# Down projection of a conv FFN: gate products of the finished accumulators moved from POOL to VectorE, and the second pair's weight blocks requested earlier

## The chip, the cores and the metric

The kernel runs on one core of one Trainium2 chip. The metric is the device time of one execution in microseconds (us), as a median over runs. The engines are named as in the profile: PE (TensorE, matrix products), PEld (its weight loads), DVE (VectorE), ACT (ScalarE), POOL (GpSimd) and SP (SyncE, which here only issues transfers). A DMA is a transfer between memory in HBM (also the kernel's own scratch there) and SBUF. PSUM holds the accumulators of PE, eight banks of 128 x 512 fp32.

## The reference, cut to what matters

One layer over 512 positions and 1024 channels, all in fp32. The part around the change is the second sub-layer and what closes it:

```
def _conv_ffn(h, w_up, conv_w, conv_b, w_down):
    z = h @ w_up                                   # 512 x 5632
    ...
    zc = conv_b + conv_w[0] * zp[:, 0:S]           # causal, width 3
    ...
    val, gate = jnp.split(zc, 2, axis=-1)
    return (jax.nn.silu(gate) * val) @ w_down      # 2816 -> 1024
...
y = _conv_ffn(h, w_up[l], conv_w[l], conv_b[l], w_down[l])
x = _layer_norm(ALPHA * x + gt_f[:, None, :] * y) * ln_f_g[l] + ln_f_b[l]
```

`gt_f` is a gate per channel, computed from the condition `c`. In the kernel it lies as two row tiles, `gt_f[0]` and `gt_f[1]` (128 x 512, the same row in all partitions; in the trace `gtf`).

## The kernel before, in words

Products in near fp32: each operand is split into a high part (a copy to fp32r by ACT, names ending in h) and a low part (the difference, by DVE, names ending in l). A product is hi x hi + lo x hi + hi x lo, three matrix products. In a sweep the products with the low part of the weights are called the rests; they come after the others (line 1599, against 1601 and 1602).

Up projection: 44 units (`m`) of 128 rows of `w_up`, two to a pass `i` (value and gate). ACT, DVE and POOL apply convolution, Silu (ACT, line 1582) and the product val x gate (POOL, line 1583). Two passes make a pair `p` of 256 rows of `w_down`, 11 pairs in all (`HP`). `first_left` and `other_lefts` make the left factors (`xa xs xh xl` for the first sweep, `yh yl ys` for the second; the latter go to scratch in HBM for nine pairs).

Down projection: a scheme with seven block products in place of eight per 2 x 2 blocks. The first sweep accumulates four of them over the pairs (`m1 m5 m6 m7`, two row halves each, eight banks), the second the other three (`m2 m3 m4`). The weights of a pair of the first sweep are two raw blocks of 128 x 512 (`db0`, `db1`: the outer ones, for `m1`, `m7`) and a wide one of 128 x 1024 (`da`: the inner one, for `m6`, `m5`). For each, SP requests the raw tile, ACT casts it (`dbh`, `dah`), DVE subtracts (`dbl`, `dal`, line 1514), PE multiplies. Cast and difference tiles have two buffers each, so a cast waits until PE is done with the block but one before. The second sweep has `dc` (wide) and `dd`, in the same way, for pairs 0 to 4; pairs 5 to 10 (`R2 = 6`) have their three blocks split ahead and kept (`second_weights`: raw tiles `dr`, results `d2.. d3.. d4..` with the pair's number). `reload` fetches a pair's left factors back from scratch into `z` tiles, on POOL's queue. The list `ahead` says which of these follow which pair of the first sweep, as space allows (`free`).

Between the sweeps the eight banks are summed into SBUF tiles `u1 u4 u3 c22` (`evacuate`). Each belongs to a quarter of the output: `fold` multiplies it by `gt_f` (POOL, line 1704) and adds it to ALPHA * x (`residual`, DVE, line 1696). The row statistics follow for those that are then complete (line 1701). The closing (`close`, `final`, `row_end`) ends `m2 m3 m4` with the six pairs kept, row half by row half, multiplies by the gate, adds, normalizes and stores.

A scheduler sets each engine's order: it issues in the order of its own timeline, within the program's data dependencies. `behind_split` forbids it to place work ahead of the last split recorded in `last_lo`. Engines work in order: an instruction that waits holds up all behind it.

Of the kernel before, what the change touches and what calls it, by code (L numbers as in the profile page):

```python
# [17 lines left out]
D = 1024  # L18
# [33 lines left out]
def trunk(ctx: ExitStack, tc: tile.TileContext, A, out):  # L52
# [1456 lines left out]
    def split_wide(parts, n, name):  # L1509
        hi = wp.tile([P, D], F32R, name=name + "h", tag="whi")  # L1510
        lo = wp.tile([P, D], F32R, name=name + "l", tag="wlo")
        for raw, c in parts:
            nc.scalar.copy(out=hi[:, c], in_=raw)
            nc.vector.tensor_tensor(out=lo[:, c], in0=raw, in1=f(hi[:, c]), op=ALU.subtract)  # L1514
        return hi, lo
# [20 lines left out]

    def first_weights(p):
        rb = [block(wdn_row(2 * p, lo_half), "db0"), block(t3_t[p], "db1")]
        ra = whole(wide_t[p], "da")
        wb_ = split_wide(zip(rb, (lo_half, hi_half)), D, "db")  # L1540
        wa_ = split_wide(((ra, slice(0, D)),), D, "da")
        return wb_, wa_

    held = [None]
    for i in range(NP):
        half = []
        for v in range(2):
# [9 lines left out]
            if m == 2 * NP - 1:  # L1557
                opening = first_weights(0)
            cc = C_CONV + 4 * m
# [12 lines left out]
            half.append(t)  # L1572
        val, gate = half
        if 3 <= i < 3 + KT:
            ada_wide_piece(3, i - 3)
# [57 lines left out]
    for i in range(R2 - 2):  # L1633
        ahead += [(second_weights, HP - R2 + 2 + i, act_t), (reload, i)]
    ahead.append((reload, R2 - 2))
    free = 1 + 6
    for p in range(HP - 1):
        wb_, wa_ = first_weights(p) if p else opening
        x = lefts1(p)
        sweep_step(p, (  # L1640
            (wb_, ((m1, x[1], lo_half), (m7, x[7], hi_half))),
            (wa_, ((m6, x[6], lo_half), (m5, x[5], hi_half))),
        ))
        for _ in range(2 if p else 0):
            need = 6 if ahead and ahead[0][0] is second_weights else 3
            if ahead and free >= need:
                work, *args = ahead.pop(0)
                work(*args)
                free -= need
        free += 4  # L1650
    p = HP - 1
    rb = [block(wdn_row(2 * p, lo_half), "db0"), block(t3_t[p], "db1")]
    ra = whole(wide_t[p], "da")
    ws1 = {
# [48 lines left out]
    def fold(t, n, u):  # L1703
        nc.gpsimd.tensor_tensor(out=u, in0=u, in1=gt_f[n], op=ALU.mult)
        residual(t, n, u)
# [10 lines left out]
    for p in range(HP - R2):  # L1716
# [8 lines left out]
        ))  # L1725
        if R2 - 1 + p < SPILLED:
            reload(R2 - 1 + p)
        if p == 0:
            fold_whole(0)
            fold_whole(1)  # L1730
        if p == 1:
            fold(0, 0, u1[0])
            fold(1, 0, u1[1])
        if p == 2:
            fold(0, 1, u4[0])
            fold(1, 1, u4[1])
            lnfg = row_tiles(4, h_t, "lnfg")
            lnfb = row_tiles(5, h_t, "lnfb")
        if p == 3:
            fold(2, 0, u3[0])  # L1740
            fold(3, 0, u3[1])
    second_weights(HP - R2, h_t, pad_t)
    closing = [HP - 5, HP - 4, HP - 2, HP - 1, HP - 3, HP - 6]

    def final(t, n, acc, op, slot):
        q = pt_t("fq")
        nc.vector.tensor_tensor(out=q, in0=acc, in1=gt_f[n], op=ALU.mult)  # L1747
        nc.vector.tensor_tensor(out=x1[t][n], in0=x1[t][n], in1=q, op=op)  # L1748
        statistics(t, slot, n)
# [45 lines left out]
    for t in range(2):  # L1795
        close(2, m2[t], t)
        final(t, 0, m2[t], ALU.add, 0)
        close(3, m3[t], t)
        final(t, 1, m3[t], ALU.add, 1)
        row_end(t, 2)  # L1800
        if t == 0:
            close(4, m4[0], 0)
            final(2, 0, m4[0], ALU.subtract, 1)
            row_end(2, 2)
# [114 lines left out]
```

## Time and profile before

| what | value |
|---|---|
| median of three runs | 954.65 us (954.14 to 956.67) |
| the profiled execution | 952.53 us, span of its instructions 950.8 us |
| mean granted PE clock | 0.994 |
| first sweep | 823 to 888 us |
| second sweep | 888 to 917 us |
| closing and output | 917 us to the end |

The span runs from the first to the last instruction. "Idle before" in brackets behind a row of the timeline says how long the engine stood still before it and what ended that. A number before an engine's name in a row is its start, then its duration. `x2` at a row's end means two instructions merged in one row. The rows that matter are shown where the prediction uses them.

### The profile page before, as it was taken

The numbers are of one execution on the slowest core, as the hardware profiler recorded it, in microseconds if no ns is written. First come the engines' busy times: TensorE is split into PE (matmuls) and PEld (weight loads), VectorE is DVE, ScalarE is ACT, GpSimd is POOL, SyncE is SP. The second block draws the span as 40 slices with busy tenths as digits, with TensorE's granted clock in tenths as the row PEclk, the third lists the DMA queues.
The fourth block names the chain that finished last, engine by engine and source line by source line (L and its number), as shares of the span: only waits on it lengthen the run. The fifth ranks groups of instructions, "written<-read, shape, count | busy, mean of one in ns | idle before, by whom it ended". The sixth has DMA issues, their size and how long they took to land. (4 is left out here: it accounts for less than half of the span.)

```text
span 950.8 us, 12652 instructions
## 1 busy us (share of the span) xinstructions
PE 925.1 (97%) x4456; PEld 779.7 (82%) x4456; DVE 683.8 (72%) x1048; ACT 409.0 (43%) x690; POOL 282.1 (30%) x340
## 2 busy tenths in 40 slices
PE   7999999999999999999999999999999999989796
PEld 6988888888888888888888889988888888778585
DVE  7966668546677798776375689588887656667868
ACT  4576555533324322133323434655444455555221
POOL 4741121122342154402154713022213221111704
PEclk9999999999999999999999999999999999999898
DMA  9823112134447996774576440155554444399832
GB/s 333 314 68 105 58 35 83 42 135 154 135 144 270 327 356 226 255 239 137 174 261 205 154 156 23 46 182 194 178 171 141 146 143 144 122 320 326 288 95 89
DMA packets 68303, 165.78 MB, mean 174 GB/s; under 512 B 9232, under 2 KB 12752, under 8 KB 68240
## 3 DMA queue, kind: packets, MB, share of 16 engines
q1 hardware_dynamic: 57024, 137.54, 43.2%
q0 software_dynamic: 10784, 26.89, 8.1%
q8 instruction: 35, 0.57, 0.2%
q10 hardware_dynamic: 432, 0.55, 0.2%
q14 instruction: 28, 0.23, 0.1%
HBM read 144.16 MB, written 20.78 MB: 173 GB/s over the span
## 5 line engine op out<-in xcount | busy, mean ns | idle before, releaser
L95 DVE TENSOR_TENSOR wupl<-wup,wuph 128x1024 fp32r<-128x1024 f32 x38 | 52.4, 1379 | 24.1 <-PE pzu L118 15.9
L1583 POOL TENSOR_TENSOR zc<-zc 128x512 f32<-128x512 f32 x22 | 29.7, 1349 | 131.5 <-ACT zc L1582 108.0
L94 ACT CAST wuph<-wup 128x1024 fp32r<-128x1024 f32 x38 | 40.1, 1054 | 46.4 <-PE pzu L116 33.8
L94 ACT CAST wbh<-wb 128x1024 fp32r<-128x1024 f32 x24 | 25.3, 1054 | 71.7 <-PE py L116 53.0
L985 POOL DMA_DIRECT2D wt<-wb x44 | 24.4, 556 | 78.3 <-DVE wb L981 73.3
L95 DVE TENSOR_TENSOR wgl<-wg,wgh 128x1024 fp32r<-128x1024 f32 x22 | 29.9, 1359 | 20.7 <-PE pg L118 9.9
L1561 ACT ACTIVATE zc<-pzu,cols 128x512 f32<-128x512 f32 x44 | 34.0, 778 | 21.0 <-PE pzu L118 16.6
L981 DVE TENSOR_TENSOR wb<-wb,wb 128x512 f32<-128x512 f32 x44 | 35.3, 806 | 6.1 <-DMA wb<-in_wdn 5.7
L856 DVE SCALAR_TENSOR_TENSOR ada<-adar,cact,ada 128x512 f32<-128x512 f32 x42 | 38.6, 960 | 0.0
L95 DVE TENSOR_TENSOR wbl<-wb,wbh 128x1024 fp32r<-128x1024 f32 x24 | 30.9, 1288 | 10.7 <-PE pg L118 5.3
L775 POOL TENSOR_SCALAR pe<-pe,mx 128x128 f32<-128x128 f32 (+3 forms) x32 | 17.0, 534 | 69.3 <-DVE mx L774 52.4
L94 ACT CAST wgh<-wg 128x1024 fp32r<-128x1024 f32 x22 | 23.3, 1059 | 32.6 <-PE pg L116 24.7
L1564 DVE SCALAR_TENSOR_TENSOR zc<-pzu,cols,zc 128x511 f32<-128x511 f32 x44 | 32.5, 743 | 5.0 <-ACT zc L1561 4.9
L1568 DVE SCALAR_TENSOR_TENSOR zc<-pzu,cols,zc 128x510 f32<-128x510 f32 x44 | 32.6, 744 | 0.7
L419 POOL TENSOR_TENSOR mg<-mg,th 128x512 f32<-128x512 f32 x16 | 28.5, 1778 | 12.7 <-DVE th L416 12.5
L1623 POOL DMA_DIRECT2D z<-ys x27 | 14.7, 545 | 52.3 <-PE pd L1602 24.3
L298 DVE SCALAR_TENSOR_TENSOR acc<-ada,cact,acc 128x256 f32<-128x256 f32 (+1 forms) x29 | 28.7, 990 | 1.0
L937 POOL TENSOR_TENSOR asum<-apad 128x527 f32<-128x527 f32 x8 | 12.3, 1543 | 54.6 <-ACT apad L932 28.0
L1582 ACT ACTIVATE zc<-zc 128x512 f32<-128x512 f32 x22 | 13.9, 631 | 24.2 <-DVE zc L1568 24.2
L1160 POOL TENSOR_TENSOR oraw<-oraw,gtt 128x512 f32<-128x512 f32 x6 | 9.6, 1612 | 42.2 <-DMA oraw<-in_wo 42.2
L1182 POOL TENSOR_TENSOR o<-o,gtt 128x512 f32<-128x512 f32 x10 | 17.9, 1809 | 12.4 <-DMA o<-in_wo 10.9
L771 ACT ACTIVATE pe<-sc,mx 128x128 f32<-128x128 f32 (+3 forms) x32 | 16.8, 528 | 8.7 <-DVE mx L769 7.5
(1570 smaller groups left out, 3247.6 us busy)
## 6 DMA issues: line engine op xcount, KB each, us to landing
wup<-in_wup SPq DMA_DIRECT2D x44, 512.0 KB, 3.5
wb<-in_wb SPq DMA_DIRECT2D x24, 512.0 KB, 3.8
adar<-in_ada SPq DMA_DIRECT2D x48, 256.0 KB, 4.2
wg<-in_wg SPq DMA_DIRECT2D x22, 512.0 KB, 3.5
wb<-in_wdn SPq DMA_DIRECT2D x44, 256.0 KB, 5.0
wt<-wb POOLq DMA_DIRECT2D x44, 256.0 KB, 3.8
z<-ys POOLq DMA_DIRECT2D x27, 256.0 KB, 6.1
ada<-in_ada1p SPq DMA_DIRECT2D x24, 256.0 KB, 4.8
```

Source lines behind the costliest of these rows:

```text
L94: nc.scalar.copy(out=hi[:, :n], in_=raw[:, :n])
L95: ins = nc.vector.tensor_tensor(out=lo[:, :n], in0=raw[:, :n], in1=f(hi[:, :n]), op=ALU.subtract)
L298: ins = nc.vector.scalar_tensor_tensor(out=acc, in0=src, scalar=cact[:, k : k + 1], in1=acc, op0=ALU.mult, op1=ALU.add)
L419: nc.gpsimd.tensor_tensor(out=merged[m], in0=merged[m], in1=th, op=ALU.add)
L856: nc.vector.scalar_tensor_tensor(out=acc[n], in0=src, scalar=cact[:, k : k + 1], in1=acc[n], op0=ALU.mult, op1=ALU.add,)
L981: ins = nc.vector.tensor_tensor(out=dst, in0=x, in1=y, op=op)
L985: nc.gpsimd.dma_start(out=dst, in_=src)
L1182: nc.gpsimd.tensor_tensor(out=halves[n], in0=halves[n], in1=gt[n], op=ALU.mult)
L1561: nc.scalar.activation(t, pz, AF.Identity, bias=cols[:, cc + 3 : cc + 4], scale=cols[:, cc + 2 : cc + 3])
L1564: nc.vector.scalar_tensor_tensor(out=t[:, 1:512], in0=pz[:, 0:511], scalar=cols[:, cc + 1 : cc + 2], in1=t[:, 1:512], op0=ALU.mult, op1=AL ...
L1568: nc.vector.scalar_tensor_tensor(out=t[:, 2:512], in0=pz[:, 0:510], scalar=cols[:, cc : cc + 1], in1=t[:, 2:512], op0=ALU.mult, op1=ALU.add,)
L1583: nc.gpsimd.tensor_tensor(out=val, in0=val, in1=gate, op=ALU.mult)
```

## The change

Four things, all from the last up unit on. The raw outer blocks of pair 1 are requested together with pair 0's, and their split is written ahead of the last Silu. In the first sweep the weights kept for the second start after pair 2 in place of pair 1, at most one pair's per step, and all but two of the reloads are written before the second sweep. The gate products of `fold` go from POOL to DVE; they are written behind each pair's rests by `behind_split` (five of the eight), and three accumulators of the first row half and of the third quarter (`u1[0]`, `u4[0]`, `u3[0]`) are no longer folded there: `final` adds the second-sweep accumulator to them, multiplies the sum and adds it to ALPHA * x, four DVE instructions where there were three. The norm's rows (`lnfg`, `lnfb`) lie in tiles of another pool.

```diff
--- before.py
+++ after.py
@@ -1511,7 +1511,8 @@
         lo = wp.tile([P, D], F32R, name=name + "l", tag="wlo")
         for raw, c in parts:
             nc.scalar.copy(out=hi[:, c], in_=raw)
-            nc.vector.tensor_tensor(out=lo[:, c], in0=raw, in1=f(hi[:, c]), op=ALU.subtract)
+            ins = nc.vector.tensor_tensor(out=lo[:, c], in0=raw, in1=f(hi[:, c]), op=ALU.subtract)
+        last_lo[:] = [ins.ins]
         return hi, lo
 
     def whole(src, name):
@@ -1534,12 +1535,19 @@
     def wdn_row(k, c):
         return A["wdn"][k * P : (k + 1) * P, c]
 
-    def first_weights(p):
-        rb = [block(wdn_row(2 * p, lo_half), "db0"), block(t3_t[p], "db1")]
-        ra = whole(wide_t[p], "da")
-        wb_ = split_wide(zip(rb, (lo_half, hi_half)), D, "db")
-        wa_ = split_wide(((ra, slice(0, D)),), D, "da")
-        return wb_, wa_
+    def outer_raws(p):
+        return [block(wdn_row(2 * p, lo_half), "db0"), block(t3_t[p], "db1")]
+
+    def outer_split(raws):
+        return split_wide(zip(raws, (lo_half, hi_half)), D, "db")
+
+    def inner_raw(p):
+        return whole(wide_t[p], "da")
+
+    def inner_split(raw):
+        return split_wide(((raw, slice(0, D)),), D, "da")
+
+    opening = {}
 
     held = [None]
     for i in range(NP):
@@ -1555,7 +1563,10 @@
                 pz = ps("pzu")
                 mm_chunk(pz, uh, ul, h2_hi, h2_lo)
             if m == 2 * NP - 1:
-                opening = first_weights(0)
+                raws = outer_raws(0)
+                inner = inner_raw(0)
+                raws1 = outer_raws(1)
+                opening[0] = outer_split(raws), inner_split(inner)
             cc = C_CONV + 4 * m
             t = pt_t("zc")
             nc.scalar.activation(
@@ -1571,6 +1582,8 @@
             )
             half.append(t)
         val, gate = half
+        if i == NP - 1:
+            outer1 = outer_split(raws1)
         if 3 <= i < 3 + KT:
             ada_wide_piece(3, i - 3)
         if i == 3 + KT:
@@ -1632,25 +1645,33 @@
     ahead = [(second_weights, HP - R2 + 1, h_t)]
     for i in range(R2 - 2):
         ahead += [(second_weights, HP - R2 + 2 + i, act_t), (reload, i)]
-    ahead.append((reload, R2 - 2))
+    ahead += [(reload, i) for i in range(R2 - 2, R2 + 1)]
     free = 1 + 6
     for p in range(HP - 1):
-        wb_, wa_ = first_weights(p) if p else opening
+        if p == 0:
+            wb_, wa_ = opening[0]
+        else:
+            wb_ = outer1 if p == 1 else outer_split(outer_raws(p))
+            wa_ = inner_split(inner_raw(p))
         x = lefts1(p)
         sweep_step(p, (
             (wb_, ((m1, x[1], lo_half), (m7, x[7], hi_half))),
             (wa_, ((m6, x[6], lo_half), (m5, x[5], hi_half))),
         ))
-        for _ in range(2 if p else 0):
-            need = 6 if ahead and ahead[0][0] is second_weights else 3
-            if ahead and free >= need:
-                work, *args = ahead.pop(0)
-                work(*args)
-                free -= need
+        wide = 0
+        while p > 1 and ahead:
+            weights = ahead[0][0] is second_weights
+            need = 6 if weights else 3
+            wide += weights
+            if free < need or wide > 1:
+                break
+            work, *args = ahead.pop(0)
+            work(*args)
+            free -= need
         free += 4
     p = HP - 1
-    rb = [block(wdn_row(2 * p, lo_half), "db0"), block(t3_t[p], "db1")]
-    ra = whole(wide_t[p], "da")
+    rb = outer_raws(p)
+    ra = inner_raw(p)
     ws1 = {
         c: split_block(raw, f"d{c}", h_t)
         for c, raw in ((1, rb[0]), (7, rb[1]), (6, ra[:, :512]), (5, ra[:, 512:]))
@@ -1701,7 +1722,7 @@
         return nc.vector.bn_stats(out=stats[t][:, slot, :], in_=x1[t][n][:, c])
 
     def fold(t, n, u):
-        nc.gpsimd.tensor_tensor(out=u, in0=u, in1=gt_f[n], op=ALU.mult)
+        nc.vector.tensor_tensor(out=u, in0=u, in1=gt_f[n], op=ALU.mult)
         residual(t, n, u)
 
     def fold_whole(t):
@@ -1723,29 +1744,30 @@
             (wc_, ((m2, x[2], lo_half), (m3, x[3], hi_half))),
             (wd_, ((m4, x[4], lo_half),)),
         ))
-        if R2 - 1 + p < SPILLED:
-            reload(R2 - 1 + p)
-        if p == 0:
-            fold_whole(0)
-            fold_whole(1)
-        if p == 1:
-            fold(0, 0, u1[0])
-            fold(1, 0, u1[1])
+        if R2 + 1 + p < SPILLED:
+            reload(R2 + 1 + p)
+        if p in (1, 2):
+            behind_split(fold_whole, p - 1)
         if p == 2:
-            fold(0, 1, u4[0])
-            fold(1, 1, u4[1])
-            lnfg = row_tiles(4, h_t, "lnfg")
-            lnfb = row_tiles(5, h_t, "lnfb")
+            lnfg = row_tiles(4, act_t, "lnfg")
+            lnfb = row_tiles(5, act_t, "lnfb")
         if p == 3:
-            fold(2, 0, u3[0])
-            fold(3, 0, u3[1])
+            behind_split(fold, 3, 0, u3[1])
+            behind_split(fold, 1, 0, u1[1])
+        if p == 4:
+            behind_split(fold, 1, 1, u4[1])
     second_weights(HP - R2, h_t, pad_t)
     closing = [HP - 5, HP - 4, HP - 2, HP - 1, HP - 3, HP - 6]
 
-    def final(t, n, acc, op, slot):
+    def final(t, n, acc, op, slot, u=None):
         q = pt_t("fq")
-        nc.vector.tensor_tensor(out=q, in0=acc, in1=gt_f[n], op=ALU.mult)
-        nc.vector.tensor_tensor(out=x1[t][n], in0=x1[t][n], in1=q, op=op)
+        if u is None:
+            nc.vector.tensor_tensor(out=q, in0=acc, in1=gt_f[n], op=ALU.mult)
+            nc.vector.tensor_tensor(out=x1[t][n], in0=x1[t][n], in1=q, op=op)
+        else:
+            nc.vector.tensor_tensor(out=q, in0=u, in1=acc, op=op)
+            nc.vector.tensor_tensor(out=q, in0=q, in1=gt_f[n], op=ALU.mult)
+            residual(t, n, q)
         statistics(t, slot, n)
 
     def row_end(t, count):
@@ -1794,13 +1816,13 @@
     last_product.clear()
     for t in range(2):
         close(2, m2[t], t)
-        final(t, 0, m2[t], ALU.add, 0)
+        final(t, 0, m2[t], ALU.add, 0, None if t else u1[0])
         close(3, m3[t], t)
-        final(t, 1, m3[t], ALU.add, 1)
+        final(t, 1, m3[t], ALU.add, 1, None if t else u4[0])
         row_end(t, 2)
         if t == 0:
             close(4, m4[0], 0)
-            final(2, 0, m4[0], ALU.subtract, 1)
+            final(2, 0, m4[0], ALU.subtract, 1, u3[0])
             row_end(2, 2)
     halves = (slice(0, 256), slice(256, 512))
     close(4, m4[1][:, :256], 1, halves[0])
```

On ACT, at the last up unit (`zc` from `pzu` is the unit's bias step, `zc<-zc` its Silu, `yh xs xh ys` the last pair's left factors); before:

```order
L1561 ACTIVATE zc<-pzu,cols 128x512
L1582 ACTIVATE zc<-zc 128x512
L1481 CAST yh_7686<-zc 128x512
L1458 CAST xs_7683<-se 128x256
L1479 CAST xh_7684<-sd 128x512
L1513 CAST dbh<-db_7729 128x512
L1513 CAST dah<-da 128x1024
L1458 CAST ys_7688<-se 128x256
L1513 CAST dbh<-db_7731 128x512
```

and now:

```order
L1572 ACTIVATE zc<-pzu,cols 128x512
L1513 CAST dbh<-db_7661 128x512
L1513 CAST dbh<-db_7663 128x512
L1595 ACTIVATE zc<-zc 128x512
L1481 CAST yh_7696<-zc 128x512
L1458 CAST xs_7693<-se 128x256
L1513 CAST dah<-da 128x1024
L1479 CAST xh_7694<-sd 128x512
```

Both outer casts of pair 1 moved ahead of Silu, its wide cast ahead of one left factor.

On ACT, a few pairs later (`d27h d37h d47h` are pair 7's kept blocks); before, from pair 2's wide cast:

```order
L1513 CAST dah<-da 128x1024
L1530 CAST d27h<-dr_7827 128x512
L1530 CAST d37h<-dr_7829 128x512
L1530 CAST d47h<-dr_7831 128x512
L1513 CAST dbh<-db_7851 128x512
L1513 CAST dbh<-db_7853 128x512
L1513 CAST dah<-da 128x1024
```

and now, from pair 3's outer casts:

```order
L1513 CAST dbh<-db_7827 128x512
L1513 CAST dbh<-db_7829 128x512
L1513 CAST dah<-da 128x1024
L1531 CAST d27h<-dr_7867 128x512
L1513 CAST dbh<-db_7891 128x512
L1513 CAST dbh<-db_7893 128x512
L1531 CAST d37h<-dr_7869 128x512
L1531 CAST d47h<-dr_7871 128x512
```

Pair 3's casts stood behind pair 7's kept blocks and now stand ahead of them; the two later kept blocks stand between pair 4's outer casts and its wide one.

On DVE, in the second sweep from the last sums of the evacuation on (`c_` is a c22 tile, `x_..` the residual, `std` the statistics); before:

```order
L1685 TENSOR_TENSOR u_8248<-pd_7699,u_8248 128x512
L1696 SCALAR_TENSOR_TENSOR x_00_5043<-x_00_5043,u_8238 128x512
L1684 TENSOR_TENSOR c_8274<-pd_7700,u_8263 128x512
L1685 TENSOR_TENSOR u_8253<-pd_7700,u_8253 128x512
L1696 SCALAR_TENSOR_TENSOR x_10_5047<-x_10_5047,u_8243 128x512
L1514 TENSOR_TENSOR dcl<-dc,dch 128x1024
L1531 TENSOR_TENSOR d25l<-dr_8484,d25h 128x512
L1514 TENSOR_TENSOR ddl<-dd,ddh 128x512
L1696 SCALAR_TENSOR_TENSOR x_21_5052<-x_21_5052,c_8268 128x512
```

and now:

```order
L1705 TENSOR_TENSOR c_8286<-pd_7710,u_8275 128x512
L1706 TENSOR_TENSOR u_8265<-pd_7710,u_8265 128x512
L1514 TENSOR_TENSOR dcl<-dc,dch 128x1024
L1514 TENSOR_TENSOR ddl<-dd,ddh 128x512
L1725 TENSOR_TENSOR c_8280<-c_8280,gtf_7075 128x512
L1717 SCALAR_TENSOR_TENSOR x_21_5052<-x_21_5052,c_8280 128x512
L1722 BN_STATS std_8245<-x_21_5052 128x6
L1532 TENSOR_TENSOR d25l<-dr_8478,d25h 128x512
L1514 TENSOR_TENSOR dcl<-dc,dch 128x1024
L1514 TENSOR_TENSOR ddl<-dd,ddh 128x512
```

Pair 1's split (the first `dcl` here) stood behind two residuals whose products came from POOL; now both residuals are later or in the closing, and the products (line 1725) stand behind a pair's splits.

## The prediction

> **What bounds the kernel now.** I read the page first, then the chain of waits from 640 us on, then the timelines of the engines around the waits it names.
>
> ```profile
> span 950.8 us, 12652 instructions
> ...
> PE 925.1 (97%) x4456; PEld 779.7 (82%) x4456; DVE 683.8 (72%) x1048; ACT 409.0 (43%) x690; POOL 282.1 (30%) x340
> ```
>
> ```profile
> PE pe L1599 <- DVE dcl L1514: 6.2, 1, 6.2
> ...
> PE pd L1601 <- ACT dbh L1513: 4.4, 2, 2.6
> ```
>
> TensorE (PE) is busy for 97% of the span, and in the last 310 us it waits three times: twice for ScalarE's split of a first-sweep block (dbh), once for VectorE's split of a second-sweep block (dcl). Between them it has no idle time, so a wait removed is time gained, unless another takes its place. The prices come from starts in PE's timeline:
>
> ```profile
> 823.18 0.39 PE L1601 MATMUL pd<-dbh,xa 128*128 128x512 f32 x1
> ...
> 830.61 0.50 PE L1601 MATMUL pd<-dbh,xa 128*128 128x512 f32 x1 [1.83 <-ACT dbh L1513]
> ...
> 836.58 0.39 PE L1601 MATMUL pd<-dbh,xa 128*128 128x512 f32 x1
> ...
> 844.79 0.50 PE L1601 MATMUL pd<-dbh,xa 128*128 128x512 f32 x1 [2.61 <-ACT dbh L1513]
> ...
> 855.98 0.39 PE L1601 MATMUL pd<-dbh,xa 128*128 128x512 f32 x1
> ...
> 888.62 0.39 PE L1601 MATMUL pe<-dch,z 128*128 128x512 f32 x1
> ...
> 892.70 0.39 PE L1601 MATMUL pe<-dch,z 128*128 128x512 f32 x1
> ...
> 901.75 2.07 PE L1599 MATMUL pe<-dcl,z 128*128 128x512 f32 x4 [6.17 <-DVE dcl L1514]
> ...
> 904.47 0.46 PE L1601 MATMUL pe<-dch,z 128*128 128x512 f32 x1
> ```
>
> These are starts of pairs 0, 1, 2, 3 and 5 of the first sweep, then pairs 0, 1 (its rests at 901.75) and 2 of the second. From 855.98 to 888.62 six pairs take 32.64, 5.44 each; from 888.62 to 892.70 a second-sweep pair takes 4.08. Against that pairs 0 and 1 lose 13.40 - 10.88 = 2.52, pair 2 to 3 loses 8.21 - 5.44 = 2.77, pairs 3 and 4 lose 11.19 - 10.88 = 0.31, and second-sweep pair 1 loses 11.77 - 4.08 = 7.69. All losses: 13.29 us.
>
> The last loss is the 6.17 wait and a slow restart: windows of four microseconds give the granted clock (PEclk) behind it.
>
> ```profile
> core 0: us, PE busy (x) PEld busy (x) DVE busy (x) ACT busy (x) POOL busy (x), PEclk, DMA share, GB/s
> 896.00:900.00 4.00, 0.00 (x0) 0.00 (x0) 4.00 (x2) 0.00 (x0) 4.00 (x4) 0.72 0.25 80
> 900.00:904.00 4.00, 2.25 (x5) 1.82 (x6) 4.00 (x5) 1.67 (x2) 2.76 (x5) 0.50 0.55 163
> 904.00:908.00 4.00, 4.00 (x18) 3.22 (x17) 4.00 (x7) 1.40 (x2) 1.08 (x2) 0.92 1.04 309
> ```
>
> At half clock the six rests took 2.72 instead of 1.36. Why the block was late stands in VectorE's timeline beside POOL's:
>
> ```profile
> 889.91 2.75 DVE L1696 SCALAR_TENSOR_TENSOR x<-x,u 128x512 f32<-128x512 f32 x1 [0.49 <-POOL u L1704]
> ...
> 893.79 5.71 DVE L1696 SCALAR_TENSOR_TENSOR x<-x,u 128x512 f32<-128x512 f32 x1
> 899.42 2.28 DVE L1514 TENSOR_TENSOR dcl<-dc,dch 128x1024 fp32r<-128x1024 f32 x1
> ...
> 902.82 0.68 DVE L1696 SCALAR_TENSOR_TENSOR x<-x,c 128x512 f32<-128x512 f32 x1
> 903.42 0.68 DVE L1696 SCALAR_TENSOR_TENSOR x<-x,u 128x512 f32<-128x512 f32 x1
> ...
> 904.63 1.20 DVE L1514 TENSOR_TENSOR dcl<-dc,dch 128x1024 fp32r<-128x1024 f32 x1
> ```
>
> ```profile
> 888.57 2.55 POOL L1704 TENSOR_TENSOR u<-u,gtf 128x512 f32<-128x512 f32 x2
> ...
> 892.74 1.31 POOL L1704 TENSOR_TENSOR c<-c,gtf 128x512 f32<-128x512 f32 x1
> 894.00 2.51 POOL L1704 TENSOR_TENSOR u<-u,gtf 128x512 f32<-128x512 f32 x2
> ...
> 897.68 2.92 POOL L1704 TENSOR_TENSOR u<-u,gtf 128x512 f32<-128x512 f32 x2
> ```
>
> The same residual takes 0.68 once POOL has stopped multiplying, but 2.75 and 5.71 while it multiplies. The split queued behind is itself slow (2.28 against 1.20) and ends at 901.70; PE's rests start at 901.75.
>
> **The change part by part.** *Products.* POOL loses eight multiplications; VectorE gets five of them in the second sweep and three in the closing. A VectorE product of two fp32 SBUF tiles with gtf is not in the trace. Its nearest row is the residual at 902.82, with as many operands of the same size: 0.68, the next one starting 0.60 later; the far end is 5.71, beside a multiplying POOL. I take 0.60, or 0.72 where an instruction needs the one before it, since POOL then multiplies nothing. The cover is VectorE's spare time in a pair: between pair 1's wide split and pair 2's come a 512-wide split 0.60, product 0.60, residual 0.72, statistics 0.72, the split d25l 0.60, and pair 2's wide split 1.20, which is 4.4 against PE's 4.08 (statistics taken as long as the residual). The next two rounds, up to pair 4's wide split, hold 3.9 and 4.8. So the lead counts. Pair 1's wide split follows ScalarE's cast of the same block:
>
> ```profile
> 891.31 1.05 ACT L1513 CAST dch<-dc 128x1024 fp32r<-128x1024 f32 x1 [6.89 <-PE pe L1602]
> ```
>
> It can end at 892.36 + 1.20 = 893.6 and is wanted after 12 of the pair's 18 products, at 892.70 + 2.72 = 895.4. Carried through the rounds, the leads are 1.9, 1.5, 1.7 and 1.0. VectorE stays ahead and the 7.69 goes.
>
> *Second pair's blocks.* ScalarE reached pair 1's dbh only behind a cast that waited for POOL:
>
> ```profile
> 828.29 0.62 ACT L1481 CAST yh<-zc 128x512 fp32r<-128x512 f32 x1 [1.46 <-POOL zc L1583]
> ...
> 829.95 0.61 ACT L1513 CAST dbh<-db 128x512 fp32r<-128x512 f32 x1
> ...
> 841.12 0.62 ACT L1530 CAST d27h<-dr 128x512 fp32r<-128x512 f32 x1 [4.42 <-DMA dr<-in_wdn]
> ...
> 844.12 1.13 ACT L1513 CAST dbh<-db 128x512 fp32r<-128x512 f32 x2
> ```
>
> Now both halves stand ahead of the last Silu. Their buffer is free after pair 0's first eight products (0.227 each), about 825.2, so they end at 826.3; PE wants them near 828. Silu, which waits behind them, moves by some 0.1, and with it POOL's product and the last pair's left factors, which PE needs 50 us later. Pair 1's dah, behind two of those casts, ends near 830.6 and is wanted 36 products after 823.18, at 831.3. On SP the two requests pass ahead of wide loads for pairs 1 and 2: two issues of some 0.5 (below, 1.13 for two), hidden, as pair 1's wide block is not cast before 829. The 2.52 goes.
>
> *Second-sweep weights later.* The 844.12 cast for pair 3 stood behind d27h, which waited 4.42 for a transfer. Now pair 3's casts stand ahead of d27h, pair 4's dbh behind it. Next to be late: PE reaches pair 4 at 823.18 + 4 x 5.44 = 844.9 and its wide block at 846.8, whose cast stands behind d47h. The requests cannot go out earlier than before, since they wait for raw tiles that the d26 to d46 splits free:
>
> ```profile
> 834.57 1.13 SPq L1524 DMA_DIRECT2D dr<-in_wdn  x2
> ```
>
> Here 6.55 passed from issue to use. With 7 to 8 for the third, d47h ends near 845.5 and the wide cast near 846.5: a lead of 0.3. The cost lies between nothing and the old 2.77. I take 0.7 for all narrow places of pairs 4 to 6, the 0.31 of today within it, because order and lead both say that at most a part comes back. On POOL's queue the last reloads lose the products in front of them; the last norm's rows move on SP behind the last blocks, where only output stores follow. Both cost nothing.
>
> *Closing.* Three accumulators get four dependent instructions instead of three.
>
> ```profile
> 921.11 0.69 DVE L1747 TENSOR_TENSOR fq<-pe,gtf 128x512 f32<-128x512 f32 x1 [5.60 <-PE pe L110]
> ...
> 930.39 1.44 DVE L1748 TENSOR_TENSOR x<-x,fq 128x512 f32<-128x512 f32 x1
> ...
> 937.43 0.69 DVE L1747 TENSOR_TENSOR fq<-pe,gtf 128x512 f32<-128x512 f32 x1 [0.54 <-PE pe L110]
> ```
>
> ```profile
> 929.99 1.29 POOL L1769 TENSOR_TENSOR x<-x,lnfb 128x512 f32<-128x512 f32 x1 [1.14 <-ACT x L1768]
> ```
>
> The first added one falls in PE's shadow (VectorE waits 5.60 around it). The other two push a queue that from 927 to the end idles only those 0.54: 2 x 0.72 - 0.54 = 0.9, and 0.2 for meeting POOL's remaining adds, as the 1.44 at 930.39 did (0.75 more than 0.69): 1.1 in all. Ends: 0.6 (pitch 0.60, no new meeting) and 2.4 (two new ones).
>
> By the Trainium skill, "SBUF — State Buffer", Who interferes with whom, a VectorE instruction with two SBUF inputs and a POOL instruction that reads SBUF exclude each other, the later one waiting to the end of the earlier. The 1.44 agrees; the 5.71 spans several multiplications and is longer than that rule gives. By it any of the three four-step chains that meets an add waits it out; that is rival (5).
>
> **Sum.** 13.29 - 0.7 - 1.1 = 11.5. The profiled execution took 952.53 (span 950.8 and 1.7 around it) and would take 941.0; the median, 954.65, lies 2.1 higher, so 943.1.
>
> **The rivals.** (1) The stall only moves: d47h lands late and pair 4 waits what pair 3 did. For it: a lead of 0.3 beside a wait of 4.42. Against: only half of pair 4 stands behind it. 2.77 in place of 0.7: 945.2.
> (2) Transfers become the limit.
>
> ```profile
> 824.00:908.00 84.00, 73.28 (x314) 58.98 (x313) 62.98 (x80) 40.32 (x63) 26.25 (x36) 0.96 0.91 304
> 844.00:872.00 28.00, 27.21 (x119) 22.29 (x120) 18.14 (x25) 17.47 (x27) 3.22 (x6) 1.00 1.00 351
> 884.00:896.00 12.00, 11.58 (x52) 9.24 (x50) 11.51 (x12) 2.62 (x4) 9.02 (x11) 1.00 1.13 397
> ```
>
> The 84 us move 25.5 MB at 304 GB/s (last column), at a 0.91 share. Of these some 1.5 MB can go before or after. The other 24 have 84 - 12.6 = 71.4 us; at the 351 held for 28 us they need 68.4. If only 304 is held they need 78.9: 950.2. I price the middle, 946.6.
> (3) VectorE falls behind in the second sweep: were each of its ten products and residuals 0.35 longer, 3.5 less the last lead of 1.0 would be lost: 945.6. The leads speak against it.
> (4) Slower than before: the long residuals were not POOL's doing but the transfers', which fill the engines just there (884 to 896: share 1.13, 397 GB/s). Then each of the ten in the second sweep costs the mean excess of the two, (2.07 + 5.03) / 2 = 3.55, and 35.5 - 1.0 come on top: 978. It ends above 954.65 from an excess of 1.3 each. Against it: the 5.71 runs on through 896 to 900, where the share is 0.25, and residuals take 0.68 again from 902.82 while the share climbs to 1.04; both long ones lie beside POOL's products. The Trainium skill, "SBUF — State Buffer", SBUF: two separate sides, has transfers and engines on separate ports; the rows at 896 and 904 agree.
> (5) The closing is dearer: all three four-step chains meet one of POOL's adds, which stay, at 0.75 each as at 930.39: 2.3 more, 945.4. For it: VectorE is full there. Against: one meeting stands in the trace for three adds beside it.
>
> **How the numbers follow.** Forecast 0.56, own range 941.3 to 944.7; rivals (1) 0.16, (2) 0.10, (3) 0.06, (4) 0.04, (5) 0.05; 0.03 for a change that takes its gain back elsewhere and ends within 0.3% (2.9 us, about what a measurement here tells from no change), where the far end of (2) also lies, 0.01. Range 940.8 to 947.5: below, all 13.29 less 0.6 and a run's scatter; above, rivals (1), (3) and (5) and the middle of (2). Faster 0.92, same 0.04, slower 0.04.
>
> **What would show it.** Right: no PE wait over 0.5 before pair 1, the residuals at 0.6 to 0.75, the second sweep's PE without a gap, granted clock 1.00 to the closing, the closing's first fq near 909. Wrong: a PE wait for dbh or dah at pair 4 with a cast on ScalarE waiting for dr (1); waits for z or dc transfers (2); PE waiting for dcl with POOL idle (3) or residuals above 2 (4); more than 2.4 us longer from first fq to the end (closing).

## The result, and the profile after

The changed kernel took 940.73 us (median of four runs, 940.67 to 941.47) against 955.66 for the kernel before beside it: a ratio of 0.9844, 95% interval 0.9822 to 0.9866. The forecast was 943.1 in a range from 940.8 to 947.5: the sign was right, the forecast 2.4 too high, and the median lies 0.07 below the range. Two later comparisons of the same pair gave 942.44 (ratio 0.9881, 0.9862 to 0.9901) and 940.73 (0.9857, 0.9837 to 0.9878). Over all twelve runs the median is 941.14 (939.85 to 944.20), over all 43 runs of the kernel before 954.07 (952.26 to 957.8): 12.9 less.

The page of the changed kernel:

```profile
span 939.0 us, 12633 instructions
...
PE 922.3 (98%) x4456; PEld 778.8 (83%) x4456; DVE 679.2 (72%) x1053; ACT 408.7 (44%) x690; POOL 270.1 (29%) x332
```

Its waits of PE from 640 us on (us in total, how often, the longest). There were three; one is left, for another block:

```profile
PE pd L1614 <- ACT dah L1513: 1.1, 1, 1.1
```

PE's timeline (L1614 and L1612 are 1601 and 1599 of before): starts of pairs 0, 5 and 6 of the first sweep with the wait in pair 5, then pairs 0 and 1 of the second sweep, pair 1's rests, pair 2, and the closing.

```profile
822.42 0.39 PE L1614 MATMUL pd<-dbh,xa 128*128 128x512 f32 x1
...
849.62 0.39 PE L1614 MATMUL pd<-dbh,xa 128*128 128x512 f32 x1
...
853.63 0.50 PE L1614 MATMUL pd<-dah,xh 128*128 128x512 f32 x1 [1.12 <-ACT dah L1513]
...
856.50 0.39 PE L1614 MATMUL pd<-dbh,xa 128*128 128x512 f32 x1
...
883.70 0.39 PE L1614 MATMUL pe<-dch,z 128*128 128x512 f32 x1
...
887.78 0.39 PE L1614 MATMUL pe<-dch,z 128*128 128x512 f32 x1
...
890.50 1.07 PE L1612 MATMUL pe<-dcl,z 128*128 128x512 f32 x4
...
891.86 0.39 PE L1614 MATMUL pe<-dch,z 128*128 128x512 f32 x1
...
903.65 0.39 PE L108 MATMUL pe<-d26l,z 128*128 128x512 f32 x1
```

Five pairs take 27.20, that is 5.44 a pair: pairs 0 to 4 together lose nothing. Pair 5 takes 6.88 and loses 1.44. In the second sweep each pair takes 4.08, and pair 1's rests follow at once. VectorE there:

```profile
887.48 1.23 DVE L1514 TENSOR_TENSOR dcl<-dc,dch 128x1024 fp32r<-128x1024 f32 x1 [1.78 <-ACT dch L1513]
...
889.23 0.68 DVE L1725 TENSOR_TENSOR c<-c,gtf 128x512 f32<-128x512 f32 x1
889.94 0.69 DVE L1717 SCALAR_TENSOR_TENSOR x<-x,c 128x512 f32<-128x512 f32 x1
...
892.01 1.22 DVE L1514 TENSOR_TENSOR dcl<-dc,dch 128x1024 fp32r<-128x1024 f32 x1
...
908.38 0.69 DVE L1768 TENSOR_TENSOR fq<-u,pe 128x512 f32<-128x512 f32 x1 [4.16 <-PE pe L110]
...
918.98 1.66 DVE L1717 SCALAR_TENSOR_TENSOR x<-x,fq 128x512 f32<-128x512 f32 x1
```

A product takes 0.68, a residual 0.69. Pair 1's split ends at 888.71, 1.8 before it is wanted at 890.50 (forecast: 1.9). The granted clock (third column from the end) stays at 1.00; the last column has the GB/s that the transfers move:

```profile
884.00:888.00 4.00, 4.00 (x19) 3.31 (x18) 2.22 (x4) 1.30 (x2) 1.78 (x4) 1.00 1.21 397
888.00:892.00 4.00, 4.00 (x19) 3.33 (x18) 3.90 (x6) 2.47 (x4) 1.74 (x4) 1.00 1.03 298
892.00:896.00 4.00, 4.00 (x20) 3.30 (x19) 3.93 (x8) 1.57 (x2) 0.94 (x2) 1.00 1.09 355
```

The span divides at three starts in the timelines of PE and VectorE: pair 0 of the first sweep, pair 0 of the second, and the closing's first fq.

| kernel (number of profiled executions) | start of first sweep | first sweep | second sweep to first fq | fq to end |
|---|---|---|---|---|
| before, the one shown | 823.18 | 65.44 | 32.49 | 29.69 |
| before, mean of 5 | 823.66 | 65.54 | 32.99 | 29.70 |
| after, the one shown | 822.42 | 61.28 | 24.68 | 30.62 |
| after, mean of 3 | 822.99 | 61.02 | 24.68 | 30.61 |
| products alone | 822.65 | 64.49 | 24.68 | 30.58 |
| opening alone | 823.01 | 60.76 | 33.17 | 29.76 |
| ahead alone | 823.71 | 65.33 | 33.80 | 29.66 |

The means differ by 12.6: 4.5 in the first sweep, 8.3 in the second, 0.9 given back in the closing, and 0.7 ahead of the first sweep, where the program is the same and its start varies from 822.4 to 824.8 between executions.

### The profile page after: what moved, and what is told of

Same layout as the page of the kernel before. It is cut to its first block, busy times and chain, and to the rows that moved or that the text cites. A ratio compares the mean times of both kernels' runs of the same rounds, so it can differ in the third digit from the quotient of the medians.

```text
span 939.0 us, 12633 instructions
## 1 busy us (share of the span) xinstructions
PE 922.3 (98%) x4456; PEld 778.8 (83%) x4456; DVE 679.2 (72%) x1053; ACT 408.7 (44%) x690; POOL 270.1 (29%) x332
## 4 chain that ended last, share of the span: by engine, by line
PE 97%; DVE 1%; POOL 0%; ACT 0%; DMA 0%; issue 0%; POOLq 0%; SPq 0%; ACTq 0%
PE pzu L115 7%; PE pzu L116 7%; PE pzu L118 7%; PE py L115 5%; PE py L116 5%; PE py L118 5%; PE pg L115 4%; PE pg L116 4%; PE pg L118 4%; PE lat L528 2%; PE pd L1614 2%; PE pd L1612 2%; PE pd L1615 2%; PE pa L115 2%; PE pu L115 2%; PE pu L116 2%
```

## The experiments

**The parts alone.** Three kernels are the kernel before with one part of the diff each; a fourth is the kernel before again. Only the gate products on VectorE, with `final` and the norm's rows:

```diff
-        nc.gpsimd.tensor_tensor(out=u, in0=u, in1=gt_f[n], op=ALU.mult)
+        nc.vector.tensor_tensor(out=u, in0=u, in1=gt_f[n], op=ALU.mult)
...
+            behind_split(fold_whole, p - 1)
```

> The kernel before with the third part alone: the gate products on VectorE behind each pair's rests, three of them in the closing; the first sweep as before. Both theories take the second sweep's loss (7.7 us in the profile of before) away and add 0.9 in the closing. Theory A (the 2 to 3 us by which the runs of before exceed its profiled run, and their spread of 3.7 us, are VectorE held up by POOL's products for a time that differs from run to run): 9 to 10 us faster in the median and runs within 1 us of each other. Theory B (they come from transfers landing at other times in the first sweep): 6.8 us faster, and the spread of before stays.

Only pair 1's outer blocks (`raws1`, `outer1`):

```diff
+                raws1 = outer_raws(1)
...
+            outer1 = outer_split(raws1)
```

> The kernel before with the second pair's raw blocks requested and split ahead of the last Silu, nothing else. Both theories: PE's wait before pair 1 goes, 2.5 us faster. Theory A: the runs spread as those of before do (3 us or more). Theory B: part of the spread goes.

Only the list and loop of the second-sweep weights, with the reloads:

```diff
-    ahead.append((reload, R2 - 2))
+    ahead += [(reload, i) for i in range(R2 - 2, R2 + 1)]
...
+        while p > 1 and ahead:
```

> The kernel before with the kept second-sweep weights one pair later and the reloads moved ahead, nothing else. Both theories: PE's wait of 2.6 us before pair 3 goes, up to 2.8 us faster; less if, as in the changed kernel, a kept block's transfer holds ScalarE up at a later pair (1.1 us there). Theory A: the spread of before stays. Theory B: the spread goes, since the wait for that transfer is where it comes from.

And the kernel before, once more:

> The kernel before once more, for a second profile of it. Theory A: the starts of the first sweep's pairs agree with the first profile to 0.3 us, and the second sweep's loss differs from 7.7, between 8 and 13 us if this run is slower. Theory B: the losses differ before pair 5, and the second sweep loses 7.7 again.

Beside 953.88 for the kernel before they took 945.34 (ratio 0.9908, 0.9891 to 0.9925), 949.34 (0.9950, 0.9935 to 0.9965), 953.78 (1.0001, 0.9989 to 1.0013), and the copy 954.38 in one run: 8.5, 4.5 and 0.1, together 13.1 against the 12.9 of the whole. The parts add up, and one of them is worth nothing that these runs show. The 8.5 of the products lies between the 6.8 of theory B and the 9 to 10 of theory A. With them alone PE has one wait left from 640 us on:

```profile
PE pd L1602 <- ACT dbh L1513: 1.8, 1, 1.8
```

The one at pair 3 is absent there, as it is in three of the five profiled executions of the kernel before; these have one of 0.91 to 1.03 at pair 4 in its place, and why this kernel has none no run says. With the opening alone the one for dcl stays, and both for dbh are gone, pair 3's too:

```profile
PE pe L1611 <- DVE dcl L1514: 6.3, 1, 6.3
PE pd L1613 <- ACT dah L1513: 0.6, 1, 0.6
```

ScalarE's timeline of that kernel gives the reason: pair 3's wide cast now stands ahead of d27h, though `ahead` is as before.

```profile
838.62 1.05 ACT L1513 CAST dah<-da 128x1024 fp32r<-128x1024 f32 x1 [0.18 <-PE pd L1614]
842.98 0.62 ACT L1530 CAST d27h<-dr 128x512 fp32r<-128x512 f32 x1 [3.30 <-DMA dr<-in_wdn]
```

With pair 1's blocks earlier, the scheduler puts pair 3's casts ahead of d27h by itself. With "ahead" alone it does not: pair 3's casts still stand behind d47h, as in the kernel before.

```profile
843.05 0.62 ACT L1530 CAST d47h<-dr 128x512 fp32r<-128x512 f32 x1 [0.43 <-DMA dr<-wt]
843.58 1.14 ACT L1513 CAST dbh<-db 128x512 fp32r<-128x512 f32 x2
```

In the copy the third wait is 6.17 again, to the hundredth, so a varying hold-up between VectorE and POOL was not what spreads the runs; pair 2 to 3 lost 3.63 there against 2.77.

**Nothing from "ahead".** The changed kernel with the list, loop and reloads of before, beside the changed kernel itself:

```diff
-    ahead += [(reload, i) for i in range(R2 - 2, R2 + 1)]
+    ahead.append((reload, R2 - 2))
```

> The changed kernel without its part on the second-sweep weights (the list and loop of before, reloads as before). ScalarE's order is then that of the changed kernel, row for row; three reloads on POOL's queue and the norm's rows on SP stand elsewhere. Theory O: the earlier blocks of pair 1 alone remove the wait of pair 3, and this part adds nothing: 940.7, within 0.5 of the changed kernel, and one PE wait near 1.1 at pair 5. Theory of the prediction: this part removes the 2.77, so it comes back: 943.5, with a PE wait above 2 at pair 3.

> The changed kernel again, in more runs, for the step that added 2.1 us to the profiled execution's forecast. Theory W: the runs of the kernel before differ because ScalarE stands in order behind transfers that land at other times from run to run, and with those waits gone the runs lie close: median 940.4 to 941.2, all of ten runs or so within 1.5 us. Theory S: the four runs so far lay close by chance; more runs spread as those of the kernel before do (3.8 us over 17 runs), with a median of 941.5 to 943.1.

942.04 (940.7 to 942.84) and 942.44 (940.8 to 944.2). Theory O holds: PE waits for dah once, 1.5 and 0.8, and nothing comes back at pair 3. The first sweep with the old list took 62.00, against 60.55 to 61.81 in eight profiled executions that have the new one and the opening, so some tenths from this part are not excluded. And theory S holds: the first four runs lay close by chance.

**The wait that is left.** The casts and differences of the kept weights written behind the next pair's split:

```diff
+        for args in pending:
+            behind_split(second_splits, *args)
...
+            if weights:
+                pending.append((*args, second_raws(args[0])))
```

> The changed kernel with the casts and differences of the kept second-sweep weights written behind the next pair's split; their raw tiles are requested where they were. Theory: the 1.12 us that PE still waits at pair 5 comes from dah standing behind d38h, which waits 2.04 for its transfer; with d38h behind the next pair's outer casts it goes: 939.6, no PE wait over 0.3 in the first sweep. Rival: the raw tiles are held for a pair longer, so later requests go out later and the wait turns up elsewhere: 940.7 to 943.

941.39 (941.11 to 943.52). The wait did not go, it changed its block:

```profile
PE pd L1614 <- ACT dbh L1513: 0.9, 1, 0.9
```

**The engine or the place.** First the products on VectorE where the kernel before had them on POOL; then the reverse, the five of the second sweep on POOL in the new places.

```diff
-        if p in (1, 2):
-            behind_split(fold_whole, p - 1)
+        if p == 0:
+            fold_whole(0)
+            fold_whole(1)
...
```

> The changed kernel with the gate products on VectorE, but written where the kernel before had them (not held behind a pair's split), and a closing of three steps throughout. Theory E (POOL's multiplications made the residuals long): residuals and products 0.60 to 0.75 throughout, though the order is worse: counted at 0.6 each, pair 1's dcl ends 0.6 late, its ddl 1.5 more, pair 2's dcl and ddl 1.0 and 1.6 more, 4.7 in all, less 0.9 in the closing: 944.5. Rival T (the transfers there made them long): residuals of 2 to 5 us again, a wait of 6 or more for dcl: 947 or above.

```diff
-        nc.vector.tensor_tensor(out=u, in0=u, in1=gt_f[n], op=ALU.mult)
+        nc.gpsimd.tensor_tensor(out=u, in0=u, in1=gt_f[n], op=ALU.mult)
```

> The changed kernel with the five products that stand in the second sweep back on POOL, in their new places behind a pair's split; the closing stays at three four-step chains. If places alone did it: 941 to 942. If the engine counts: each residual waits for its product on POOL (1.3 each) with the next pair's split behind it, and the splits beside a product are longer; the leads of 0.9 to 1.8 are used up in one to three rounds: 942.5 to 946, with PE waits for dcl.

The first took 944.99 (0.9913, 0.9896 to 0.9930), as theory E counted. Its VectorE works without a gap, products and residuals 0.6 apart:

```profile
890.72 1.22 DVE L1514 TENSOR_TENSOR dcl<-dc,dch 128x1024 fp32r<-128x1024 f32 x1
...
894.87 1.29 DVE L1717 SCALAR_TENSOR_TENSOR x<-x,u 128x512 f32<-128x512 f32 x2
```

and PE still waits 2.2 for dcl: 0.20 before pair 1's rests, since five products and two residuals stand ahead of that split, and 1.97 before pair 2's, which has three more products and four residuals in front of it. The transfers are as dense there (last column) as beside the long residuals of the kernel before, whose same two windows move 403 and 388 GB/s:

```profile
888.00:892.00 4.00, 3.80 (x18) 2.82 (x16) 4.00 (x7) 1.72 (x3) 1.60 (x3) 1.00 1.18 381
892.00:896.00 4.00, 4.00 (x17) 3.06 (x18) 4.00 (x7) 1.68 (x2) 1.10 (x3) 1.00 1.19 399
```

The second took 944.26 (0.9890, 0.9870 to 0.9910); VectorE's first wide split there, beside four multiplications:

```profile
889.37 4.00 DVE L1514 TENSOR_TENSOR dcl<-dc,dch 128x1024 fp32r<-128x1024 f32 x1 [1.78 <-ACT dch L1513]
```

Neither (the opening alone) took 949.34, engine alone 944.99, place alone 944.26, both 941.14: the whole gain takes both. (The second has the shorter closing of before, worth 0.9; in the third the three products of the closing stay on VectorE.)

**POOL's multiplications by themselves.** The changed kernel with eight multiplications added on POOL that nobody waits for:

```diff
+        if p == 0:
+            beside = h_t("beside", F32)
+            for i in range(8):
+                nc.gpsimd.tensor_tensor(out=beside, in0=u4[0], in1=gt_f[i % 2], op=ALU.mult)
```

> The changed kernel with eight multiplications of 128x512 on POOL added in the second sweep (u4 of the first row half by gtf, into a spare tile that nobody reads, no wait of any other instruction on them). VectorE's instructions and their order up to pair 3 stay. If POOL's multiplications are what held VectorE: products, residuals and wide splits beside them take 2 to 6 us in place of 0.68 and 1.2; in the kernel before three of them took 8.2 more, the leads here are 1.4 to 1.8, so PE waits 3 to 7 for dcl: 944.5 to 948.5. If not (the transfers, or only the order): all at 0.6 to 1.3, no PE wait over 0.5 in the second sweep, 941 to 942.

947.29 (947.15 to 947.35; 0.9925, 0.9908 to 0.9942), 6.2 above the 941.14 of the changed kernel, and 6.0 of it between the second sweep's start and the first fq (30.72 against 24.68). VectorE, then POOL:

```profile
888.07 2.42 DVE L1514 TENSOR_TENSOR dcl<-dc,dch 128x1024 fp32r<-128x1024 f32 x1 [1.78 <-ACT dch L1513]
...
895.78 2.28 DVE L1514 TENSOR_TENSOR dcl<-dc,dch 128x1024 fp32r<-128x1024 f32 x1
...
899.67 1.76 DVE L1725 TENSOR_TENSOR c<-c,gtf 128x512 f32<-128x512 f32 x1
901.47 1.66 DVE L1717 SCALAR_TENSOR_TENSOR x<-x,c 128x512 f32<-128x512 f32 x1
```

```profile
888.09 1.31 POOL L1752 TENSOR_TENSOR beside<-u,gtf 128x512 f32<-128x512 f32 x1
...
893.99 8.58 POOL L1752 TENSOR_TENSOR beside<-u,gtf 128x512 f32<-128x512 f32 x5
```

Each of these VectorE instructions became about one multiplication longer (1.0 to 1.2). That shows that POOL's multiplications hold VectorE up and make PE wait. It does not yet show the 5.71: here the two engines took turns, in the unbroken row of five from 893.99 on too. All eight write one tile, so the next run gave them four tiles in turn:

```diff
-            beside = h_t("beside", F32)
+            beside = [h_t(f"beside{i}", F32) for i in range(4)]
```

> As the run with eight multiplications added on POOL, but they write four tiles in turn, so that none waits for the one ahead of it, and the first four stand without a request between them. Theory of the gap: in the run before each wrote the same tile, which left a gap after each in which VectorE came in, so the instructions alternated (1.7 to 2.4 each); without it the wide split of pair 1 waits for several, as the residuals of 5.71 and 6.73 did: 4 to 6 for it, 945 to 949. Rival: they alternate again, 2.3 to 2.5 for that split, and the long residuals come from their own kind of instruction: near 947.3.

948.73 (948.13 to 949.23; 0.9935, 0.9901 to 0.9969). The same split, then POOL beside it:

```profile
888.23 6.02 DVE L1514 TENSOR_TENSOR dcl<-dc,dch 128x1024 fp32r<-128x1024 f32 x1 [1.78 <-ACT dch L1513]
894.17 1.78 DVE L1514 TENSOR_TENSOR ddl<-dd,ddh 128x512 fp32r<-128x512 f32 x1
```

```profile
886.00 5.03 POOL L1752 TENSOR_TENSOR beside<-u,gtf 128x512 f32<-128x512 f32 x4
...
891.61 1.27 POOL L1752 TENSOR_TENSOR beside<-u,gtf 128x512 f32<-128x512 f32 x1
...
893.97 3.11 POOL L1752 TENSOR_TENSOR beside<-u,gtf 128x512 f32<-128x512 f32 x2
```

By the Trainium skill, "SBUF — State Buffer", Who interferes with whom, a VectorE instruction with two SBUF inputs and a POOL instruction that reads SBUF exclude each other: the later one waits for the end of the earlier. The 1.0 to 1.2 of the run that took turns agree, since one multiplication takes 1.3; the 6.02 does not. The theory of the gap holds for this split: where no multiplication waits for the one ahead of it, VectorE can stay out for several (1.23 became 6.02). How many is open. It stayed out of the pause from 891.03 to 891.61, in which POOL issued a request; but the next split, 1.78 in place of 0.69, came in between the two multiplications from 893.97, though neither waits for the other. Requests of POOL by themselves cost nothing: in the changed kernel two of them run from 891.87 to 892.94 beside the split of 1.22 at 892.01.

**Closing.** Two more products and residuals behind pair 4's split, and only one four-step chain:

```diff
             behind_split(fold, 1, 1, u4[1])
+            behind_split(fold, 0, 1, u4[0])
+            behind_split(fold, 2, 0, u3[0])
```

> The changed kernel with u4 and u3 of the closing's second and third chain multiplied and added behind pair 4's split, where VectorE stands idle 4.16 us; these two chains have three steps in the closing, only the first keeps four. If the 0.93 that the closing grew by comes from these two added steps: 0.9 less from the closing's first fq to the end, 29.7 in place of 30.6, and the first fq not later: 0.9 below the changed kernel. If the two more instructions on VectorE ahead of the closing delay its first fq, or the closing is bound elsewhere: no gain.

> The changed kernel once more beside the others, for its median over more runs: its first four runs had a median of 940.73, the next four 942.44. If the spread is one of the runs and not of the chip or the hour: a median of 940.7 to 942.5 again, a spread of 2 to 4 us, and the kernel before at 953.5 to 954.5; the profiled execution then differs from the median by what is lost ahead of 60 us and at pair 5.

941.19 (939.58 to 942.61) against 940.73 (939.85 to 942.03): no difference that four runs each can show. Its profile has the shortest span of all, 937.9, with 24.67 to the first fq and 29.75 from there, 0.87 less than the changed kernel:

```profile
908.15 0.69 DVE L1770 TENSOR_TENSOR fq<-u,pe 128x512 f32<-128x512 f32 x1 [1.75 <-PE pe L110]
```

The idle time ahead of the first fq fell from 4.16 to 1.75 and still covers the added work. So the step is right by the profile and unproved by the time.

**Where the profiled execution stood.** Three more profiled executions of the kernel before, for the 2.1 us that the forecast added:

> The kernel before, one more profiled execution, for the offset of 2.1 us that the forecast carried over. Its profiled execution so far lies 1.5 below the median of 35 runs. Theory W: the offset lies in the first sweep's waits for transfers, pair 2 to 3 above all, which the change removes: the start of the first sweep at 823.2 to 823.7 as in the execution shown, but 65.9 to 66.8 from it to the second sweep in place of 65.44. Theory U: it lies ahead of the first sweep, where both kernels are alike, and had to be carried over: start at 824 or later, 65.4 to 65.6 for the sweep.

> As for the look ahead of it: theory W a sweep of 65.9 to 66.8 after a start at 823.2 to 823.7, theory U a start at 824 or later and a sweep of 65.4 to 65.6; the third wait, for dcl, at 6.2 by both.

> As for the two looks ahead of it. With the two executions profiled earlier, these give five starts and five lengths of the first sweep; their medians against 823.18 and 65.44 divide the 1.5.

They took 954.99, 953.14 and 953.05. Theory W falls: the first sweep took 65.49, 65.32, 65.32, as in the execution shown. Theory U has its signs in the first of the three alone: the sweep began at 824.76, 823.29, 822.80, against 823.18. What grew in all three is the second sweep, which neither theory had: 33.32, 33.12 and 33.48 in place of 32.49, at the same wait. PE behind that wait in the last of them:

```profile
901.25 2.07 PE L1599 MATMUL pe<-dcl,z 128*128 128x512 f32 x4 [6.17 <-DVE dcl L1514]
...
905.68 0.63 PE L1601 MATMUL pe<-dch,z 128*128 128x512 f32 x1
906.11 0.49 PE L1602 MATMUL pe<-dch,z 128*128 128x512 f32 x1
906.43 0.40 PE L1601 MATMUL pe<-dch,z 128*128 128x512 f32 x1
```

Products of 0.63 in place of 0.39 are at half clock: the window from 900 to 904 has 0.50 granted here, as in the execution shown. Here it lasts to about 906.4, 5.1 us from the restart; in the execution shown, the row at 904.47 has 0.46 already and the next 0.40: 2.9 us. Over six executions with this wait the time at half clock runs from 2.9 to 5.7, and the stretch to the first fq from 32.49 to 33.80, in the same order. By the Trainium skill, "TensorE: Matmul & The Clock Gate", Part 1, the gate judges activity in a window that runs on regardless of the program, so that the number of slow products at a kernel's start differs from run to run; these rows, behind an idle time in mid-kernel, agree.

## Why the prediction was right or wrong

**Products: right.** The dcl wait and its restart went whole: 32.49 to 24.68 is 7.81, against 7.69. Leads were forecast at 1.9, 1.5 and 1.7; the trace has 1.8, 1.35 and 1.6 (the fourth, 1.0, came out at 0.9). The mechanism is shown by itself in the runs with added multiplications. Rival (3) falls with the leads. Rival (4) falls with the run that has the products on VectorE in the old places: its windows move 381 and 399 GB/s, and residuals and products take 0.68 and 0.69. Rival (2) had transfers that hold no more than 304 GB/s; the changed kernel moves 341 from 824 to 896, and PE has no wait for z or dc; the one late transfer that reaches PE is that of d38h, below. (By its own sum, 78.9 against 71.4, rival (2) ended 7.5 above 943.1, at 950.6 and not 950.2.)

**Second pair's blocks: right, and more than its term.** The 2.52 went.

**Second-sweep weights later: wrong cause.** The 2.77 did go, but the step named the wrong part of the change: the opening alone removes it, this part alone gives 0.1, with pair 3's casts in their old place, and without it nothing returns. The order of ScalarE that the prediction read was that of the whole change; it did not say which edit made it.

**Narrow places of pairs 4 to 6: 1.44 in place of 0.7.** Pair 4, at which the lead of 0.3 was worked out, held: d47h ended at 845.67 (forecast 845.5). Pair 5 did not:

```profile
845.05 0.62 ACT L1531 CAST d47h<-dr 128x512 fp32r<-128x512 f32 x1
...
852.01 0.62 ACT L1531 CAST d38h<-dr 128x512 fp32r<-128x512 f32 x1 [2.04 <-DMA dr<-in_wdn]
852.53 1.04 ACT L1513 CAST dah<-da 128x1024 fp32r<-128x1024 f32 x1
```

That is rival (1) in kind, one pair later and half as large; in the two other profiles of this kernel the same place lost 1.14 and 0.95. So the term was too small by 0.25 to 0.74.

**Closing: near.** 0.93 more, against 1.1. Of the three chains one met an add of POOL, at 918.98 (1.66, that is 0.97 more than 0.69), not all three as in rival (5).

**Sum: 11.5 against 11.8.** Between the executions shown, 0.74 was lost at pair 5, 0.12 and 0.17 gained in the second sweep and closing, and the first sweep began 0.76 earlier, which no step had. That the sums agree so closely is luck: the 0.74 too little at pair 5 and the 0.76 that no step had cancel. For the profiled execution the prediction gives 941.0; it took 940.67.

**The step that failed is the last: "the median, 954.65, lies 2.1 higher, so 943.1".** It took the distance of one profiled execution from a median of three runs as a constant of the program and carried it over whole. The runs showed a far smaller distance for the changed kernel: its three profiled executions lie at 940.67, 940.80 and 941.49, around its median of 941.14, so 0.47 above the one shown, where the prediction added 2.1. With 0.47 the forecast would have been 941.5.

Where the 2.1 came from is found in part. The 43 runs put the median of the kernel before at 954.07, so 0.6 of the 2.1 was the draw of three runs. The other 1.5 is the execution shown, which only one of the 43 undercuts. By the means of the table, 1.1 of that is 0.5 ahead of the first sweep (common to both kernels), 0.1 in it, and 0.5 in the restart at half clock, which goes with the wait and had to be added to the gain; the last 0.4 stays open. That the first four runs lie 0.07 below the range is chance: the median of all twelve lies inside it.

## What to carry to other kernels

A VectorE instruction with two SBUF operands beside a row of POOL multiplications can be held for several of them, not only for one: price it by a range from one multiplication to the row. Here moving the work to VectorE, behind what is waited for, took both the engine and the place. An order of the whole change does not tell which edit made it: build each edit apart before a term is put down to it. A profiled execution is one draw: with a wait in it behind which the clock is slow for a varying time, ask for several before its distance from the median is added to a forecast.

## What the runs showed of the hardware beyond this

Behind a wait of only 1.83 us PE's clock was slow in some executions, not in all. Pair 1's first product in the last of the three further executions of the kernel before:

```profile
830.24 0.50 PE L1601 MATMUL pd<-dbh,xa 128*128 128x512 f32 x1 [1.83 <-ACT dbh L1513]
...
832.57 0.63 PE L1601 MATMUL pd<-dah,xh 128*128 128x512 f32 x1
...
834.68 0.40 PE L1602 MATMUL pd<-dah,xl 128*128 128x512 f32 x1
```

The clock granted in the window of four microseconds behind it (third column from the end):

```profile
832.00:836.00 4.00, 4.00 (x13) 3.12 (x13) 3.37 (x6) 2.05 (x4) 0.00 (x0) 0.67 0.91 283
```

The same window of the execution shown, and the one behind its longer wait of 2.61 at pair 3:

```profile
832.00:836.00 4.00, 4.00 (x18) 3.31 (x19) 3.74 (x6) 3.31 (x7) 0.32 (x1) 1.00 0.94 278
...
844.00:848.00 4.00, 3.21 (x14) 2.68 (x15) 3.12 (x4) 2.21 (x4) 0.00 (x0) 1.00 1.05 403
```

Pair 1 takes 7.42 in the first, 5.97 in the second. Five of the seven profiled executions with this wait were slowed (0.59 to 0.71 granted in that window). The length of the wait alone does not decide: 2.61 here and 3.48 in the copy, both at pair 3, left the clock at 1.00. The sweep did not get longer by it (65.32 against 65.44): PE then came later to the next late cast and waited 1.01 once, at pair 4, in place of 2.61 at pair 3.

The two engines need not take turns: a wide split of 1.23 us took 2.28 beside multiplications that wait for each other and 6.02 beside ones that do not.
